# Where the operands of the matrix multiplications lie: all moving ones 192 bytes past all stationary ones, modulo 512

## The chip, the cores and the metric

One NeuronCore of one Trainium2 chip runs the whole kernel. The metric is device time in microseconds (us): before the change 970.22 us, the median of 3 runs (969.55 to 970.27).

## The reference

A small decoder trunk: two layers on a sequence of 256 tokens with 1024 channels, everything in float32. With the sizes of this case (feed-forward width 2816, recurrent width 1280) it computes

```python
h = x
for i in range(2):
    h = h + 0.5 * swiglu(rms_norm(h, ffn1_norm[i]), gate, up, down)     # (silu(x@gate) * (x@up)) @ down
    hn = rms_norm(h, mix_norm[i])
    m = rglru_mixer(hn, ...) if i == 0 else pool_mixer(hn, ...)         # recurrent layer, pooling layer
    h = h + m
    h = h + 0.5 * swiglu(rms_norm(h, ffn2_norm[i]), gate, up, down)
    gate = sigmoid(rms_norm(h, ple_norm[i]) @ ple_w_gate[i])
    h = h + gate * (p[i] @ ple_w_proj[i])
return rms_norm(h, final_norm)
```

Nearly all of the arithmetic is matrix products with weights that are read once: four feed-forward blocks of three 1024 x 2816 products, the in- and out-projections of the recurrent layer, and the two gates of the per-layer input.

## The kernel before

**Layout.** The activations lie transposed, channels on the 128 partitions and the 256 tokens along the free dimension. A weight block of 128 x 128 is the stationary operand of a matmul (TensorE loads it with LDWEIGHTS), a slice of 128 channels x 256 tokens the moving one. The output of 128 x 256 is summed in a PSUM bank.

**Three products for one.** To keep float32 accuracy, each operand is split into a high part in the reduced format float32r and the float32r remainder: `wh`, `wl` for weights, `xh`, `xl` for activations. `mm3` issues three matmuls per block, (wh, xh), (wh, xl), (wl, xh). That gives 7,624 matmuls in float32r; nearly all are of 256 columns. In program order each has its own LDWEIGHTS, and the LDWEIGHTS of the next matmul runs beside the current one. All of them are recorded under one line of a helper, L294.

**The stream of weights.** The weights come as one list of units (`ORDER`), each of 128 partitions x 1024 floats (512 KB). `unit()` hands out the next one and keeps two counters ahead of it: SyncE issues the load of a unit 7 places ahead into a tile `raw` (L261, 5 buffers), and `split` makes its high part (ScalarE, L272) and its low part (VectorE, L273) 4 places ahead in a tile `hl` (6 buffers): the high part of 4096 bytes per partition, then the low one. A unit feeds 24 matmuls.

**The activations.** `Norm.put` writes the split activations into a tile `x` (7 buffers), one for each 256 channels: high and low part, each of two slices of 256 floats. In the feed-forward block the hidden values are split into a tile `hid` (2 buffers of 4096 bytes) and are moving operands of the down products (`acc`). In the recurrent layer `yr` and `ytp` are the two parts of the moving operand of the out-projection (`accl`). `ri` (the gates of the recurrence) is a plain float32 product of weights that are not split.

**Where the buffers lie.** Buffers are laid out one pool behind the other in each partition: constants, `raw`, `hl`, `h` (6 buffers of 2048 bytes), `x`, `st` (small tiles, squares), then the pools of the current stage. The tile `hl` asks for 2 x 1024 + 24 floats, so its pitch is 8288 bytes, 96 past a multiple of 512; the tile `x` asks for 1024 + 8 floats, a pitch of 4128 bytes, 32 past one. Within a tile every operand slice starts at a multiple of 512. By its start modulo 512, then, the allocation gives:

| operand | bytes past a multiple of 512 |
| --- | --- |
| stationary, the 6 buffers of `hl` | 128, 224, 320, 416, 0, 96 |
| moving, the 7 buffers of `x` | 192, 224, 256, 288, 320, 352, 384 |
| moving, `hid`, `yr`, `ytp` | 416 |

This text calls (start of the moving operand minus start of the stationary one) modulo 512 the *offset* of a matmul. It changes with the buffers that meet: in the out-projection the moving operand is always at 416, and the units 0 to 5 of its weights lie in `hl` buffers at 416, 0, 224, 320, 128 and 96, so their 24 matmuls each have the offsets 0, 416, 192, 96, 288 and 320.

**Order of the work.** The order on TensorE is the order of the program: for each normalisation, `project_all` walks over two halves of the channels of several projections; inside it two small float32 sequences are placed by hand, the sums of squares (`ss`, L341, 8 matmuls of one column) and the spreading of the scale over the partitions (`spread`, L378, 4 matmuls). Then the rest of a feed-forward block follows as gate, up and down units without a stop. At the start, 12 float32 matmuls on a tile of ones (`idle`, L241) keep TensorE busy until the first weights are there.

Of the kernel before, what the change touches and what calls it, by code (L numbers as in the profile page):

```python
# [9 lines left out]
F32 = mybir.dt.float32  # L10
F32R = mybir.dt.float32r
# [4 lines left out]
P = 128  # L16
D = 1024
S = 256
# [10 lines left out]
U = 1024  # L29
# [12 lines left out]
    _at += _w  # L42
NV = _at

LINE = 32


def lines(n):
    return -(-n // LINE) * LINE

# [71 lines left out]
def width(key):  # L122
    if key[0] == "lru_gates":
        return min(8, len(GATE_BLOCKS[key[1]]) - 8 * key[2]) * P
    if key[0] == "ple_in":
        return 2 * S
    if key[0] == "pool_op":
        return 4 * (POOL_COLS[key[1]][1] - POOL_COLS[key[1]][0])
    return U
# [81 lines left out]
def trunk(ctx: ExitStack, tc: tile.TileContext, xT, vec, w, out):  # L211
    nc = tc.nc
    PSUM = bass.MemoryType.PSUM
    const = ctx.enter_context(tc.tile_pool(name="const", bufs=1))
    rawp = ctx.enter_context(tc.tile_pool(name="raw", bufs=5))
    hlp = ctx.enter_context(tc.tile_pool(name="hl", bufs=6))
    hp = ctx.enter_context(tc.tile_pool(name="h", bufs=6))
    xp = ctx.enter_context(tc.tile_pool(name="x", bufs=7))
    st = ctx.enter_context(tc.tile_pool(name="st", bufs=1))
# [3 lines left out]
    def narrow(pool, n, dt=F32, **how):  # L223

        return pool.tile([P, lines(n)], dt, **how)[:, :n]

    vt = narrow(const, NV, name="vt")
    nc.scalar.dma_start(vt, vec)
    ones = const.tile([P, P], F32, name="ones")
# [16 lines left out]
    def vcol(name, i):  # L246
        c = VCOL[name] + i
        return vt[:, c:c + 1]
# [15 lines left out]
    def split(n, parts=1):  # L264
        if n not in raws:
            return
        raw = raws.pop(n)
        hl = hlp.tile([P, 2 * U + 24], F32R, tag="hl", name=f"hl{n}")[:, :2 * U].rearrange("p (v u) -> p v u", v=2)
        step = width(ORDER[n]) // parts
        for i in range(parts):  # L270
            c = slice(i * step, (i + 1) * step)
            nc.scalar.activation(hl[:, 0, c], raw[:, c], AF.Copy)  # L272
            nc.vector.tensor_tensor(hl[:, 1, c], raw[:, c], hl[:, 0, c].bitcast(F32), op=ALU.subtract)  # L273
        units[ORDER[n]] = hl

    def unit(*key):
        n = state["used"]
        assert ORDER[n] == key, (ORDER[n], key)
        for what, do, ahead in (("loaded", load, LOADS_AHEAD), ("split", split, SPLITS_AHEAD)):
            while state[what] < min(n + ahead + 1, len(ORDER)):  # L280
                do(state[what])
                state[what] += 1
        state["used"] = n + 1
        return units.pop(key)
# [22 lines left out]
    class Norm:  # L307
# [6 lines left out]
            self.late = None  # L314

        def put(self, j, h, square=True):
            xt = xp.tile([P, 4 * S + 8], F32R, tag="x", name=f"x{self.sid}_{j}")[:, :4 * S].rearrange("p (v c s) -> p v c s", v=2, c=2)
            for c in range(2):
                g = vcol(self.name, 2 * j + c)
                nc.scalar.activation(xt[:, 0, c], h[:, c], AF.Copy, scale=g)  # L320
                nc.vector.scalar_tensor_tensor(  # L321
                    xt[:, 1, c], h[:, c], g, xt[:, 0, c].bitcast(F32), op0=ALU.mult, op1=ALU.subtract)
            self.x[j] = xt
            if square:
                self.square(j, h)
# [505 lines left out]
    load_x(0)  # L831
    load(0, 2)
    split(0, 4)
    load_x(1)
    load(1, 2)
    split(1, 4)
    load(2)
    load(3)
# [39 lines left out]
```

## Time and profile before

| | |
| --- | --- |
| median of 3 runs | 970.22 us |
| profiled execution, whole time | 970.42 us |
| its span, first to last instruction | 968.6 us |
| around the span | 1.8 us |
| TensorE busy | 952.8 us (98%) |
| VectorE, ScalarE, GpSimd busy | 652.1, 491.5, 55.5 us |
[...]
| HBM traffic | 172.4 MB, 178 GB/s over the span |

How to read it: matmuls overlap, since one takes some 280 ns from its start to the end of its drain while the next starts after some 118 ns. So a busy TensorE says only that there was always a matmul in flight; the pace is the distance from one start to the next. A timeline row that merges n matmuls runs from the start of the first to the end of the last; the last start is 0.28 us before that end.

### The profile page before, as it was taken

What the parts mean: (1) busy time and instruction counts of PE and PEld (TensorE: products, weight loads), DVE (VectorE), ACT (ScalarE), POOL (GpSimd) and SP (SyncE); (2) the same over time, 40 slices, a digit from 0 to 9 for tenths busy, and PEclk for the clock granted to TensorE, in tenths of its full rate; (3) what the DMA queues carried; (4) which work ended last, traced back from release to release, by engine and by line L of the source; (5) the groups of instructions that cost most, each with busy time, mean ns of one, the idle gap of its engine ahead of it and who ended that gap; (6) DMA issues with size and microseconds to landing.
All of it is one profiled execution on the core that took longest, in us unless ns stands there. A gap on an engine that the chain in (4) does not pass through costs nothing.

```text
span 968.6 us, 18712 instructions
## 1 busy us (share of the span) xinstructions
PE 952.8 (98%) x7888; PEld 944.8 (98%) x7888; DVE 652.1 (67%) x853; ACT 491.5 (51%) x634; POOL 55.5 (6%) x48
## 2 busy tenths in 40 slices
PE   9999999999999999999999999999989999999997
PEld 8999999999999999999998999999989999999996
DVE  6956555597877755655579855555678855555685
ACT  7544444468785443544456444444448544444443
POOL 1000000023201000000021000000011000000020
PEclk9999999999999999999999999999998999999999
DMA  8866556554435665665545656565524765665611
GB/s 295 286 213 191 182 181 192 169 184 170 153 111 163 209 203 176 196 196 188 183 124 182 208 184 195 167 203 176 185 89 138 251 199 175 197 191 181 193 46 44
DMA packets 49188, 173.63 MB, mean 179 GB/s; under 512 B 5584, under 2 KB 6224, under 8 KB 49104
## 3 DMA queue, kind: packets, MB, share of 16 engines
q1 hardware_dynamic: 48960, 172.29, 55.3%
q8 instruction: 61, 1.00, 0.4%
q14 instruction: 23, 0.19, 0.1%
q10 hardware_dynamic: 144, 0.15, 0.1%
HBM read 171.37 MB, written 1.05 MB: 178 GB/s over the span
## 4 chain that ended last, share of the span: by engine, by line
PE 65%; issue 20%; DVE 9%; ACT 3%; DMA 1%; POOL 0%; SPq 0%; DVEq 0%; ACTq 0%; POOLq 0%
PE up0ffn L294 13%; PE gate0ffn L294 13%; PE acc0ffn L294 12%; PE up1ffn L294 6%; PE gate1ffn L294 6%; PE acc1ffn L294 6%; DVE hl L273 3%; DVE x L321 2%; PE x L294 2%; PE accl L294 1%; PE pp L294 1%; PE ri L294 1%; ACT hl L272 1%; PE ple L294 1%; DMA h<-xT 1%
## 5 line engine op out<-in xcount | busy, mean ns | idle before, releaser
L273 DVE TENSOR_TENSOR hl<-raw,hl 128x1024 fp32r<-128x1024 f32 (+1 forms) x326 | 385.6, 1201 | 234.6 <-ACT hl L272 234.6
L272 ACT ACTIVATE hl<-raw 128x1024 fp32r<-128x1024 f32 (+1 forms) x326 | 332.2, 1036 | 398.9 <-issue 97.2
L294 PE MATMUL gate1ffn<-x,hl 128*128 128x256 f32 x1056 | 130.7, 281 | 2.5 <-DVE x L321 2.2
L294 PE MATMUL gate0ffn<-x,hl 128*128 128x256 f32 x1056 | 130.5, 281 | 0.7 <-ACT hl L272 0.5
L294 PEld LDWEIGHTS gate1ffn<-x,hl 128*128 128x128 f32 x1056 | 127.0, 188 | 3.6 <-DVE x L321 3.0
L294 PE MATMUL up1ffn<-x,hl 128*128 128x256 f32 x1056 | 130.3, 281 | 0.0
L294 PE MATMUL up0ffn<-x,hl 128*128 128x256 f32 x1056 | 129.7, 281 | 0.0
L294 PEld LDWEIGHTS gate0ffn<-x,hl 128*128 128x128 f32 x1056 | 126.9, 189 | 1.5 <-ACT hl L272 0.7
L294 PE MATMUL acc0ffn<-hid,hl 128*128 128x256 f32 x1056 | 128.2, 281 | 0.0
L294 PEld LDWEIGHTS up1ffn<-x,hl 128*128 128x128 f32 x1056 | 127.3, 188 | 0.0
L294 PEld LDWEIGHTS up0ffn<-x,hl 128*128 128x128 f32 x1056 | 127.1, 189 | 0.0
L294 PE MATMUL acc1ffn<-hid,hl 128*128 128x256 f32 x1056 | 126.6, 279 | 0.0
L294 PEld LDWEIGHTS acc0ffn<-hid,hl 128*128 128x128 f32 x1056 | 126.0, 189 | 0.2 <-ACT hid L466 0.2
L294 PEld LDWEIGHTS acc1ffn<-hid,hl 128*128 128x128 f32 x1056 | 124.7, 189 | 0.0
L334 POOL TENSOR_TENSOR sacc<-sq,sq 128x512 f32<-128x512 f32 x9 | 14.7, 1637 | 832.0 <-ACT sq L329 832.0
L321 DVE SCALAR_TENSOR_TENSOR x<-h,vt,x 128x256 fp32r<-128x256 f32 x64 | 48.7, 802 | 7.1 <-ACT x L320 7.0
L294 PE MATMUL ple<-x,hl 128*128 128x256 f32 x384 | 47.2, 282 | 0.0
L294 PEld LDWEIGHTS ple<-x,hl 128*128 128x128 f32 x384 | 46.0, 188 | 0.4 <-DVE x L321 0.2
L466 ACT ACTIVATE hid<-gs 128x512 fp32r<-128x512 f32 x44 | 27.9, 633 | 16.5 <-DVE gs L464 16.5
L320 ACT ACTIVATE x<-h,vt 128x256 fp32r<-128x256 f32 x64 | 28.5, 497 | 5.9 <-DMA vt<-vec 2.7
L464 DVE TENSOR_TENSOR gs<-th,gs 128x512 f32<-128x512 f32 x44 | 30.5, 692 | 1.4
L467 DVE TENSOR_TENSOR hid<-gs,hid 128x512 fp32r<-128x512 f32 x44 | 30.1, 685 | 0.0
(132 smaller groups left out, 688.9 us busy)
## 6 DMA issues: line engine op xcount, KB each, us to landing
raw<-w SPq DMA_DIRECT2D x320, 512.0 KB, 4.2
raw<-w SPq DMA_DIRECT2D x7, 256.0 KB, 4.7
h<-xT SPq DMA_DIRECT2D x4, 256.0 KB, 6.4
out<-hg SPq DMA_DIRECT2D x3, 256.0 KB, 2.8
raw<-w SPq DMA_DIRECT2D x1, 288.0 KB, 2.6
raw<-w SPq DMA_DIRECT2D x2, 128.0 KB, 4.9
out<-hg SPq DMA_DIRECT2D x2, 128.0 KB, 2.0
vt<-vec ACTq DMA_DIRECT2D x1, 148.0 KB, 4.6
```

The source lines that it names most:

```text
L272: nc.scalar.activation(hl[:, 0, c], raw[:, c], AF.Copy)
L273: nc.vector.tensor_tensor(hl[:, 1, c], raw[:, c], hl[:, 0, c].bitcast(F32), op=ALU.subtract)
L294: nc.tensor.matmul(o, lhsT, rhs, start=self.first, stop=self.left == 0, skip_group_check=True)
L320: nc.scalar.activation(xt[:, 0, c], h[:, c], AF.Copy, scale=g)
L321: nc.vector.scalar_tensor_tensor(xt[:, 1, c], h[:, c], g, xt[:, 0, c].bitcast(F32), op0=ALU.mult, op1=ALU.subtract)
L334: nc.gpsimd.tensor_tensor(acc, self.acc, sq, op=ALU.add)
L464: nc.vector.tensor_tensor(gs, th, gs, op=ALU.mult)
L466: nc.scalar.activation(hid[:, 0], gs, AF.Copy)
L467: nc.vector.tensor_tensor(hid[:, 1], gs, hid[:, 0].bitcast(F32), op=ALU.subtract)
```

## The change

The padding goes out of the two tiles, so that both pitches become multiples of 512 (8192 and 4096 bytes), and two small tiles go in: `shift` of 32 bytes in front of the constants, and `apart` of 192 bytes in a pool of its own between `hl` and `h`. GpSimd clears both once. Nothing else of the program differs; no instruction on TensorE, VectorE, ScalarE or SyncE is added, dropped or moved.

```diff
+APART = 48
 ...
     hlp = ctx.enter_context(tc.tile_pool(name="hl", bufs=6))
+    gap = ctx.enter_context(tc.tile_pool(name="gap", bufs=1))
     hp = ctx.enter_context(tc.tile_pool(name="h", bufs=6))
 ...
+    shift = const.tile([P, 8], F32, name="shift")
+    nc.gpsimd.memset(shift, 0.0)
+    apart = gap.tile([P, APART], F32, name="apart")
+    nc.gpsimd.memset(apart, 0.0)
     vt = narrow(const, NV, name="vt")
 ...
-        hl = hlp.tile([P, 2 * U + 24], F32R, tag="hl", name=f"hl{n}")[:, :2 * U].rearrange("p (v u) -> p v u", v=2)
+        hl = hlp.tile([P, 2, U], F32R, tag="hl", name=f"hl{n}")
 ...
-            xt = xp.tile([P, 4 * S + 8], F32R, tag="x", name=f"x{self.sid}_{j}")[:, :4 * S].rearrange("p (v c s) -> p v c s", v=2, c=2)
+            xt = xp.tile([P, 2, 2, S], F32R, tag="x", name=f"x{self.sid}_{j}")
```

## Rows read from the trace of the kernel before

**Rows 1.** The page: busy time by engine, share of the span, instructions.
```profile
PE 952.8 (98%) x7888; PEld 944.8 (98%) x7888; DVE 652.1 (67%) x853; ACT 491.5 (51%) x634; POOL 55.5 (6%) x48
```

**Rows 2.** Stretches, L294 alone: length, PE (matmuls), PEld (loads), clock, DMA, GB/s.
```profile
0.00:34.00 34.00, 26.37 (x211) 25.24 (x212) 1.00 0.85 296
34.00:197.00 163.00, 163.00 (x1380) 162.96 (x1380) 1.00 0.62 196
197.00:290.00 93.00, 92.15 (x692) 88.96 (x692) 1.00 0.44 154
290.00:323.00 33.00, 31.64 (x265) 31.08 (x263) 1.00 0.64 202
323.00:501.00 178.00, 178.00 (x1505) 178.00 (x1506) 1.00 0.58 184
501.00:544.00 43.00, 39.25 (x319) 37.76 (x318) 1.00 0.51 168
544.00:716.00 172.00, 171.80 (x1455) 171.62 (x1454) 1.00 0.58 181
716.00:742.00 26.00, 21.86 (x154) 20.53 (x153) 0.87 0.38 121
742.00:757.00 15.00, 14.09 (x117) 13.70 (x116) 1.00 0.51 169
757.00:929.00 172.00, 171.80 (x1462) 171.62 (x1461) 1.00 0.60 191
929.00:968.60 39.60, 23.07 (x189) 22.30 (x187) 0.95 0.09 28
```

**Rows 3.** Timeline, PE, out-projection: start, length, operation; the second matmul of some mm3.
```profile
277.19 0.28 PE L294 MATMUL accl<-ytp,hl 128*128 128x256 f32 x1
...
280.06 0.28 PE L294 MATMUL accl<-ytp,hl 128*128 128x256 f32 x1
...
282.87 0.28 PE L294 MATMUL accl<-ytp,hl 128*128 128x256 f32 x1
...
285.25 0.28 PE L294 MATMUL accl<-ytp,hl 128*128 128x256 f32 x1
...
285.60 0.28 PE L294 MATMUL accl<-ytp,hl 128*128 128x256 f32 x1
...
288.48 0.28 PE L294 MATMUL accl<-ytp,hl 128*128 128x256 f32 x1
```

**Rows 4.** Timeline, PE: out-projection's unit 5, and 12 matmuls of an up product.
```profile
291.95 0.39 PE L294 MATMUL accl<-ytp,hl 128*128 128x256 f32 x1 [0.52 <-DVE ytp L693]
...
292.41 0.28 PE L294 MATMUL accl<-ytp,hl 128*128 128x256 f32 x1
...
294.89 0.28 PE L294 MATMUL accl<-ytp,hl 128*128 128x256 f32 x1
...
776.20 1.58 PE L294 MATMUL up1ffn<-x,hl 128*128 128x256 f32 x12
```

**Rows 5.** Timeline, PE, windows of several lengths behind ss and behind spread.
```profile
19.81 0.48 PE L294 MATMUL gate0ffn<-x,hl 128*128 128x256 f32 x2
...
19.81 1.61 PE L294 MATMUL gate0ffn<-x,hl 128*128 128x256 f32 x12
...
27.29 0.83 PE L294 MATMUL gate0ffn<-x,hl 128*128 128x256 f32 x5
...
27.29 1.51 PE L294 MATMUL gate0ffn<-x,hl 128*128 128x256 f32 x11
```

**Rows 6.** Stretches with all engines: length, PE, PEld, DVE, ACT, POOL (instructions), clock, DMA, GB/s.
```profile
757.00:929.00 172.00, 172.00 (x1466) 172.00 (x1465) 104.91 (x113) 77.71 (x88) 0.00 (x0) 1.00 0.60 191
```

**Rows 7.** Timeline of the first microseconds, GpSimd and the first weight matmuls.
```profile
0.34 0.10 POOL L870 MEMSET const-uint8-127<- 128x1 uint8 x1
0.73 0.20 POOL L230 MEMSET ones<- 128x128 f32 x1 [0.29 <-POOLq L870]
...
6.60 1.64 PE L294 MATMUL gate0ffn<-x,hl 128*128 128x256 f32 x9 [0.51 <-ACT hl L272]
```

## The prediction

> **What bounds the kernel now.** I read the page's busy times first: TensorE is busy 98% of the span, VectorE 67%, ScalarE 51% [rows 1]. Busy TensorE is no proof of a full pace, because matmuls overlap, so the second view is the table of stretches for L294 alone [rows 2]. It shows four long stretches in which TensorE does nothing but float32r matmuls and never runs dry: 34 to 197, 323 to 501, 544 to 716 and 757 to 929 us. In the last of them VectorE is busy 104.9 of 172 us and ScalarE 77.7 [rows 6], so their work is covered; weights arrive at some 190 GB/s, where the first stretch shows 296 [rows 2]. The kernel is therefore bound by the pace of one matmul behind the other: 163.0 us / 1380 = 118.1 ns, 178.0 / 1505 = 118.3, 171.8 / 1455 = 118.1, 171.8 / 1462 = 117.5. No data wait stands in these, so whatever changes the pace goes straight into the time.
>
> The third view asks whether 118 is one number. The out-projection is an experiment that the kernel makes by itself: same shapes, same moving buffers, one weight buffer after the other, each with its offset. The middle matmuls of the mm3 that open the units stand at 277.19, 280.06, 282.87, 285.60 and 288.48 us [rows 3], so 24 matmuls take
>
> - offset 0: 2.87 us, 119.6 ns each
> - offset 416: 2.81 us, 117.1 ns
> - offset 192: 2.73 us, 113.8 ns; inside the unit, 282.87 to 285.25 is 21 matmuls in 2.38 us, 113.3 ns
> - offset 96: 2.88 us, 120.0 ns.
>
> The spread follows the offset and nothing else that differs between these units. 113.3 is the lowest steady pace that I find anywhere, 120 the highest.
>
> **The catch.** Offset 192 does not always give 113.3. The first 12 up matmuls of a unit at 776.20 also have the offset 192; their last start is at 776.20 + 1.58 - 0.28 = 777.50, so 11 distances take 1.30 us, 118.2 ns [rows 4]. Unit 5 of the out-projection (offset 320, entered after a wait for VectorE) keeps 118.1 over 21 matmuls (292.41 to 294.89) [rows 4]. So at offsets of this kind there are two steady paces, 113.3 and 118, and a stream stays in the one that it came in by: the 12 at 776.20 came from another offset at 118 and did not leave it.
>
> What counts then is how streams enter. Behind the sums of squares, at offset 448 (256 away from 192), the second matmul starts at 20.01 (19.81 + 0.48 - 0.28) and the twelfth at 21.14: ten distances in 1.13 us, 113 ns, from the second matmul on [rows 5]. Behind a spread, at offset 192, the fifth starts at 27.84 and the eleventh at 28.52: six in 0.68 us, 113.3, after four slower ones [rows 5]. Both entries fall into the fast pace. After a wait for data at offset 192 I have no clean case.
>
> **The change part by part.**
>
> *The layout.* The 32 bytes of `shift` move everything behind them from 128 to 160 modulo 512; six `hl` buffers of 8192 keep all weights at 160; with 192 bytes more, `h`, `x`, `st` and the stage pools start at 352. So `x`, `hid`, `yr` and `ytp` meet `hl` at 192 in every buffer. Exceptions, by the code: the projection `pp`, whose moving operand also lies in an `hl` tile (offset 0, 96 matmuls), the pooling product `v` with weights as moving operand (offset 320, 48 matmuls), the narrow `po` (40), and `ri`, which is float32.
>
> *The pace where nothing stops it.* At 113.3 instead of the rows' pace: 4.8 x 1380 = 6.6 us; 5.0 x 1505 = 7.5, less 0.2 for the 48 `pp` among them; 4.8 x 1455 = 7.0; 4.2 x 1462 = 6.1. Sum 27.0 us. These stretches, except the first, begin right behind a spread, the entry that rows 5 show to be fast.
>
> *The pace elsewhere.* From 197 to 290, 692 less 104 `ri` is 588 matmuls; 290 to 323 has 265, 501 to 544 has 319, 742 to 757 has 117, 929 to the end 189 [rows 2]. 1478 x 4.7 = 6.9 us. The stretch from 716 to 742 is left out: clock 0.87, waits for the normalisation and `pp`, `v`, `po`. So is 0 to 34, which waits for data (DMA share 0.85).
>
> *What is given back.* Between the last `ri` and the out-projection's unit 5, 216 matmuls fill the time of the recurrence; TensorE already waits there for VectorE's `ytp`, 0.52 us by the row [rows 4], so 216 x 4.7 = 1.0 us turns into a longer wait. Entries: two for each of eight normalisations and some 15 waits, with 20 ns each until the pace is steady (the four slow distances at 27.29 add about that), 0.6 us. `pp` at offset 0: 96 x 2 ns, 0.2 us. The last spread waits for its chain with 42 matmuls in front, 0.2 us. Sum 2.0 us.
>
> *The two memsets.* They stand ahead of `ones` in GpSimd's queue. Small memsets are recorded as 0.10 us, the one of 128 columns as 0.20 us; each new one has 8 or 48 columns, so 0 to 0.2 us each. `ones` starts at 0.73 and only feeds the warm-up, while the first weight matmul waits for ScalarE until 6.60 [rows 7]; the memsets cost nothing as long as that 5 us cover stands, 0.4 us if it were gone.
>
> *VectorE, ScalarE, DMA.* Their operands move too. The rows give no pair of the same operation at two starts, so I bound this by cover: 104.9 of 172 us means that VectorE's work could grow by half before it sets the pace [rows 6]. With matmuls 4% faster, VectorE's share goes from 61 to 64%. I take 0.
>
> Together: 27.0 + 6.9 - 2.0 = 31.9 us. The profiled execution took 970.42 us (968.6 span and 1.8 around), so 938.5; the median before is 0.2 lower, which changes nothing at this size. I predict 939.
>
> The ends for the unknown, the pace at offset 192 over long stretches: 113.3 and 120.0, the two ends of rows 3. For the 5802 + 1478, some 7,300 matmuls of these stretches, the low end gives the 32 us; the high one 7,300 x (120.0 - 118.0) = 15 us more than before.
>
> [...]
>
> **Rivals.**
>
> *Mixed.* Streams entered after a wait for data fall into 118, those behind `ss` and `spread` into 113.3. For: unit 5 of the out-projection did so, at 320 [rows 4]. Against: no such case at 192. The stretch from 34 to 197 stays as it is (6.6 us), and with it some 350 matmuls between a stage's first wait and its `ss` (1.6 us): 939 + 8.2 = 947. If a fast stream could also drop out in mid-stretch, up to 962.
>
> *Nothing to gain.* Every long stream ends up in the 118 pace, or what the rows show has to do with something other than the offset, or the layout is not what I worked out. The 12 at 776.20 speak for the first, the re-entries against it. 118.0 to 117.8 on 7,300 is 1.5 us: 969.
>
> *Slower.* Weights at 160 and moving operands at 352 meet nowhere in the kernel before as float32r operands. If the conflict depended on absolute starts too, or a disturbed stream could lock into the pace of offset 0, all matmuls would run at 120: 970 + 15 = 985. It decides as soon as the mean distance is above 118.0 + 0.2. Against it: 113.3 was reached at weights starting at 224 and 416 alike (282.87 and 19.81) [rows 3, 5].
>
> **How the numbers follow.** Fast throughout 0.62 (935 to 943 us: 4 us either way for the entries, and for the stretch from 197 to 290, where it depends on VectorE); mixed 0.18 (943 to 962); nothing to gain 0.13 (967 to 972); slower 0.07 (up to 985). About 0.2% is what a measurement of this kernel can tell from no change, here 1.9 us. The first two are faster, with 0.02 of the third: 0.82; same 0.11; slower 0.07. From 934 to 962 lie the first case and nearly all of the second, 8 in 10.
>
> **What would show it.** In the table of stretches the same counts in less time: some 156 us for the 1380 matmuls of the first long stretch, 171, 165 and 166 us for the others. In the timeline, gate and up groups of 48 matmuls take 5.44 us between starts instead of 5.67. If a stretch shows 117.8, its entry went wrong: look at the wait or the `ss` in front of it. If `accl` units still differ among each other, the layout isn't what I worked out. The wait for `ytp` should grow to about 1.5 us. The prediction is wrong if the long stretches stay within 117.5 to 118.3 ns per matmul, or go up to 120.

## The result, and the profile after

The changed kernel takes 960.34 us (median of 4 runs: 956.53, 957.91, 962.77, 963.0) against 970.22: a ratio of 0.990, 95% interval 0.986 to 0.994. The profiled execution took 957.91 us, 12.5 less than the one before. Of the busy times only TensorE's has moved much; the others are within 0.7 us of those of [rows 1].

```profile
PE 937.9 (98%) x7888; PEld 929.7 (97%) x7888; DVE 651.4 (68%) x853; ACT 491.3 (51%) x634; POOL 55.6 (6%) x50
```

The layout is what the change says. The four units of the out-projection that had four paces in [rows 3] now have one: the second matmuls of their first `mm3` are 2.72 us apart each time, 113.3 ns per matmul. Three of these starts:

```profile
269.34 0.28 PE L301 MATMUL accl<-ytp,hl 128*128 128x256 f32 x1
...
272.06 0.28 PE L301 MATMUL accl<-ytp,hl 128*128 128x256 f32 x1
...
274.78 0.28 PE L301 MATMUL accl<-ytp,hl 128*128 128x256 f32 x1
```

But the long stretches, which answer to [rows 2], did not all follow. The columns are length, PE (matmuls), PEld, clock, DMA share, GB/s, for L301 alone (the former L294); the second stretch is shown in two parts.

```profile
35.00:190.00 155.00, 155.00 (x1369) 155.00 (x1369) 1.00 0.64 204
317.00:378.00 61.00, 61.00 (x521) 61.00 (x520) 1.00 0.59 183
387.00:489.00 102.00, 102.00 (x903) 102.00 (x902) 1.00 0.62 197
534.00:703.00 169.00, 169.00 (x1437) 169.00 (x1436) 1.00 0.57 181
746.00:917.00 171.00, 171.00 (x1454) 171.00 (x1453) 1.00 0.59 187
```

Divide length by matmuls: 113.2 ns in the first stretch, 117.1 and then 113.0 in the second, 117.6 in the third and fourth. (Such a quotient comes out a little low, since matmuls that only overlap the ends are counted; starts in the timeline give 113.3 and 117.8.) Every operand lies as in the first stretch, the clock is 1.00, no wait stands in any of them, and yet there are two paces. From here on *fast* is 113.3 and *slow* 117.8 at offset 192.

The entries tell the stretches apart. All but the first begin behind a spread; this is the one at 314.88 us:

```profile
314.88 0.60 PE L385 MATMUL spread<-dg,ones 128*128 128x128 f32 x4
315.24 1.66 PE L301 MATMUL up0ffn<-x,hl 128*128 128x256 f32 x12
316.74 1.58 PE L301 MATMUL gate0ffn<-x,hl 128*128 128x256 f32 x12
```

The last 12 matmuls take 1.58 - 0.28 = 1.30 us for 11 distances, 118.2 ns: the stream came in slow and stayed so for the 528 matmuls up to the `pp`. Behind these 48, which have offset 0, the timeline has

```profile
382.77 2.08 PE L301 MATMUL pp<-hl,hl 128*128 128x256 f32 x16
384.69 5.63 PE L301 MATMUL gate0ffn<-x,hl 128*128 128x256 f32 x48
390.15 2.09 PE L301 MATMUL up0ffn<-x,hl 128*128 128x256 f32 x17
```

48 matmuls in 390.15 - 384.69 = 5.46 us, 113.8 ns with the first few in it: the same stream is fast now and stays fast to the end of the stretch.

Summed from the starts in the trace, 7,487 regular distances (100 to 140 ns between two neighbouring matmuls of L301, `po` left out) fell from 883.4 to 867.7 us (118.0 to 115.9 ns), and what lies between them (waits, entries, float32 matmuls) grew by 2.9 us. These two make up the 12.5 us to within 0.3.

### The profile page after: what moved, and what is told of

It reads as the page before. It is cut to its first block, busy times and chain, and to the rows that moved or that the text cites. A ratio compares the mean times of both kernels' runs of the same rounds, so it can differ in the third digit from the quotient of the medians.

```text
span 956.0 us, 18714 instructions
## 1 busy us (share of the span) xinstructions
PE 937.9 (98%) x7888; PEld 929.7 (97%) x7888; DVE 651.4 (68%) x853; ACT 491.3 (51%) x634; POOL 55.6 (6%) x50
## 4 chain that ended last, share of the span: by engine, by line
PE 64%; issue 21%; DVE 11%; ACT 3%; DMA 0%; POOL 0%; DVEq 0%; ACTq 0%; POOLq 0%
PE up0ffn L301 13%; PE gate0ffn L301 13%; PE acc0ffn L301 12%; PE up1ffn L301 6%; PE gate1ffn L301 6%; PE acc1ffn L301 6%; DVE hl L280 3%; DVE x L328 2%; PE x L301 2%; PE accl L301 1%; PE pp L301 1%; PE ri L301 1%; ACT hl L279 1%; PE xb L301 1%; DVE t L517 1%
## 5 line engine op out<-in xcount | busy, mean ns | idle before, releaser
L280 DVE TENSOR_TENSOR hl<-raw,hl 128x1024 fp32r<-128x1024 f32 (+1 forms) x326 | 385.2, 1199 | 228.1 <-ACT hl L279 228.0
L279 ACT ACTIVATE hl<-raw 128x1024 fp32r<-128x1024 f32 (+1 forms) x326 | 332.3, 1036 | 384.2 <-issue 93.0
L301 PE MATMUL gate1ffn<-x,hl 128*128 128x256 f32 x1056 | 130.1, 281 | 3.0 <-DVE x L328 2.4
L301 PEld LDWEIGHTS gate1ffn<-x,hl 128*128 128x128 f32 x1056 | 126.5, 189 | 4.0 <-DVE x L328 3.2
L301 PE MATMUL up1ffn<-x,hl 128*128 128x256 f32 x1056 | 129.5, 281 | 0.0
L301 PE MATMUL acc1ffn<-hid,hl 128*128 128x256 f32 x1056 | 127.6, 281 | 0.0
L301 PE MATMUL gate0ffn<-x,hl 128*128 128x256 f32 x1056 | 126.7, 278 | 0.2
L301 PEld LDWEIGHTS up1ffn<-x,hl 128*128 128x128 f32 x1056 | 126.4, 189 | 0.0
L301 PEld LDWEIGHTS acc1ffn<-hid,hl 128*128 128x128 f32 x1056 | 125.8, 189 | 0.0
L301 PE MATMUL up0ffn<-x,hl 128*128 128x256 f32 x1056 | 125.4, 277 | 0.0
L301 PE MATMUL acc0ffn<-hid,hl 128*128 128x256 f32 x1056 | 124.2, 277 | 0.0
L301 PEld LDWEIGHTS gate0ffn<-x,hl 128*128 128x128 f32 x1056 | 123.3, 188 | 0.8 <-DVE x L328 0.3
L301 PEld LDWEIGHTS up0ffn<-x,hl 128*128 128x128 f32 x1056 | 122.8, 188 | 0.0
L301 PEld LDWEIGHTS acc0ffn<-hid,hl 128*128 128x128 f32 x1056 | 122.1, 188 | 0.3 <-ACT hid L473 0.2
L301 PE MATMUL ple<-x,hl 128*128 128x256 f32 x384 | 45.6, 278 | 0.2 <-DVE x L328 0.2
L301 PEld LDWEIGHTS ple<-x,hl 128*128 128x128 f32 x384 | 44.4, 188 | 0.5 <-DVE x L328 0.4
```

Source lines behind the costliest of these rows:

```text
L301: nc.tensor.matmul(o, lhsT, rhs, start=self.first, stop=self.left == 0, skip_group_check=True)
```

## The experiments

Each kernel is the changed one with the edit shown, timed beside the kernel before on the same chip (medians 969.96 to 970.47 us). Where a single time is given, the kernel ran once, profiled.

**again: the changed kernel once more.** Do the paces belong to the program or to the run? No edit.

> The changed kernel once more, unaltered. Theory A (at offset 192 there are two steady paces, 113.3 and 117.8 ns, and a stream keeps the one it entered by until something disturbs it): each long stretch is again wholly at one of the two, and which one may differ from the first profile where the stretch begins with a wait for data; the time differs from the first one by whole stretches, some 6.1 us for each of about 1370 to 1450 matmuls. Theory B (the pace is fixed by the offset of each matmul, the rest is chance): the long stretches have the same pace as in the first profile or one in between, and single distances of 113 and 118 ns are mixed.

956.96 us. From 60 to 180 us the trace has 1061 matmuls in 120 us, from 560 to 680 and 770 to 890 us 1021 each: the first stretch fast, the second slow and then fast, the third and fourth slow, as in the profile after. So the pattern of the long stretches repeats here. Two lines, 60 to 180 and 560 to 680 us:

```profile
60.00:180.00 120.00, 120.00 (x1061) 120.00 (x1061) 1.00 0.62 194
560.00:680.00 120.00, 120.00 (x1021) 120.00 (x1020) 1.00 0.60 186
```

**kick96: disturb the streams.** If a stream merely stays in the pace by which it came in, a short stretch with another offset should let it come in again. Twelve units, three in each feed-forward block, lie 96 bytes higher in their buffers: offset 96 for 24 matmuls each, which costs some 24 x 6.7 ns per unit.

```diff
+def moved(key):
+    return 24 if key[0] in ("ffn1", "ffn2") and key[2:] in (("up", 1, 1), ("gate", 3, 0), ("gate", 7, 0)) else 0
 ...
-        hl = hlp.tile([P, 2, U], F32R, tag="hl", name=f"hl{n}")
+        k = moved(ORDER[n])
+        hl = hlp.tile([P, 2 * U + 128], F32R, tag="hl", name=f"hl{n}")[:, k:k + 2 * U].rearrange("p (v u) -> p v u", v=2)
```

> As the changed kernel, but 12 of the 327 weight units (three in each feed-forward block: the last one in front of the gap-free stretch, one of pair 3, one of pair 7) lie 96 bytes further on, so their 24 matmuls each have the offset 96, whose pace is 120 ns. In the kernel before, a stream that came from offset 96 into 192 was at 113.3 within some three matmuls in all cases. Theory A: all four gap-free stretches run at 113.3; from 957.9 us of the first profile, 528 + 1440 + 1452 slow matmuls x 4.45 ns = 15.2 us less, 12 x 24 x 6.7 ns = 1.9 us more: 944.6 us, between 942 and 948, and the runs agree better than those of the changed kernel. Theory B: only the 288 moved matmuls change, 1.9 us more than the changed kernel: 958 to 965 us.

946.97 us (944.17 to 948.81), ratio 0.975 (0.972 to 0.978). In the windows 330 to 370, 560 to 680 and 770 to 890 us:

```profile
330.00:370.00 40.00, 40.00 (x341) 40.00 (x340) 1.00 0.58 187
560.00:680.00 120.00, 120.00 (x1059) 120.00 (x1058) 1.00 0.60 190
770.00:890.00 120.00, 120.00 (x1059) 120.00 (x1058) 1.00 0.61 191
```

1059 in 120 us is 113.3. The third and fourth stretches turned fast, by an edit that moves 12 of some 320 units by 96 bytes; only the first part of the second came back slow each time. Theory A, that a stream keeps its pace until it has to come in again, holds, and its rival falls: the same stretch, with the same work of the other engines around it, runs at either pace. That a stream from 96 into 192 is always fast does not hold here, and did not in the kernel before: of three entries of that kind there, the one at 740.36 us stayed at 117.8.

**kick160: the direction of the kick.** The same with 32 bytes (offset 160), which I expected to leave slow streams slow.

```diff
-    return 24 if key[0] in ("ffn1", "ffn2") and key[2:] in (("up", 1, 1), ("gate", 3, 0), ("gate", 7, 0)) else 0
+    return 8 if key[0] in ("ffn1", "ffn2") and key[2:] in (("up", 1, 1), ("gate", 3, 0), ("gate", 7, 0)) else 0
```

> The same 12 units, but 32 bytes further on in place of 96: offset 160, with a pace of 117 ns. In the kernel before, every stream that came from 160 into 192 stayed at 117.8. Theory A: all four gap-free stretches run at 117.8 from the moved units on; the changed kernel's fast ones, 1370 matmuls from 35 to 190 us and 912 from 386 to 489 us, lose 4.45 ns each less what lies before the moved unit: 966 to 969 us, 22 us over the kernel with 96 bytes. Theory B: 288 matmuls at 117, as the changed kernel, 957 to 963 us, and within 3 us of the kernel with 96 bytes.

947.16 us (945.52 to 948.7), ratio 0.976 (0.974 to 0.978): a miss by 20 us. All four long stretches are fast (1060, 1058 and 1060 matmuls from 60 to 180, 560 to 680 and 770 to 890 us), the second from its first marked unit (354 matmuls from 330 to 370 us, 113.0 ns), the third and fourth from their second; a stream that was fast came back fast from every kick. That a re-entry keeps the side on which the stream was, as I had read the 12 matmuls in [rows 4], is refuted.

**kick208.** The same with 496 bytes (124 floats, offset 208).

```diff
-    return 24 if key[0] in ("ffn1", "ffn2") and key[2:] in (("up", 1, 1), ("gate", 3, 0), ("gate", 7, 0)) else 0
+    return 124 if key[0] in ("ffn1", "ffn2") and key[2:] in (("up", 1, 1), ("gate", 3, 0), ("gate", 7, 0)) else 0
```

> The 12 weight units of the two earlier runs, now at offset 208 (24 matmuls each at 117.8 ns), which in the scan had one pace only and was followed by 113.3 at 448 in one case. Theory A (a stream keeps the pace it came in by, and the unit ahead can turn it): if 208 wipes out what came before, all gap-free stretches are at 113.3 from the first moved unit on: 957 - 15.2 + 12 x 24 x 4.45 ns = 943 us, 941 to 946. If the exit from 208 falls into 117.8, all of them are slow behind a moved unit: 966 to 969.

954.41 us (946.74 to 957.05), ratio 0.983 (0.977 to 0.988): above the expectation, though the profiled run, 946.74, is in line with it and shows all stretches fast but the first part of the second (342 matmuls from 330 to 370 us). What the three longer runs did was not profiled. A kick does not work each time: in the long stretches of the three profiles a slow stream came out of a kick fast 2 times of 4 (offset 96), 3 of 5 (160) and 2 of 4 (208). Whether that depends on the offset is not shown.

**scan: the pace of every offset.** Each group of nine unit positions of the feed-forward blocks gets another shift, 36 in all, in steps of 16 bytes and four near 192.

```diff
+    g = 9 * (2 * l + (which == "ffn2")) + (p if m == "down" else p - 2)
 ...
+    return 4 * g if g < 32 else (126, 2, 127, 1)[g - 32]
```

> As the changed kernel, but in the feed-forward blocks the weight units of each group of 144 matmuls lie 16 bytes further on than those of the group before: 36 groups pass through all 32 offsets 192, 176, 160, ... 208 in steps of 16, and then 200, 184, 196, 188. It measures the steady pace at each offset. Theory A: groups at 64, 192, 320, 448 are at 113.3 or 117.8, at 0 and 256 at 120.0, at 96 and 352 near 120; 16 bytes to the side of 192 the pace should lie between. Is there an offset with 113.3 or less that has no slow pace? Theory B gives the same list of paces, but one value for each offset, 113.3 at 192.

969.44 us. The timeline gives each pace between two groups of 48:

```profile
334.58 5.76 PE L312 MATMUL gate0ffn<-x,hl 128*128 128x256 f32 x48
340.18 5.76 PE L312 MATMUL up0ffn<-x,hl 128*128 128x256 f32 x48
...
464.78 5.61 PE L312 MATMUL up0ffn<-x,hl 128*128 128x256 f32 x48
470.22 5.87 PE L312 MATMUL acc0ffn<-hid,hl 128*128 128x256 f32 x48
...
790.39 5.92 PE L312 MATMUL up1ffn<-x,hl 128*128 128x256 f32 x48
796.15 5.84 PE L312 MATMUL acc1ffn<-hid,hl 128*128 128x256 f32 x48
```

5.60 us for 48 is 116.7 ns at offset 48; 5.44 is 113.3 at offset 448; 5.76 is 120.0 at offset 256. All of them, ns per matmul:

| offset | pace | offset | pace |
| --- | --- | --- | --- |
| 0, 256 | 120.0 | 144, 400 | 120.0 |
| 16, 272 | 120.0 | 160; 416 | 118.6; 117.3 |
| 32, 288 | 116.7 | 176, 432 | 118.8 |
| 48, 304 | 116.7 | 184; 188 | 118.3 |
| 64, 320 | 117.8 | 192, 448 | 113.3 (or 117.8) |
| 80, 336 | 118.1 | 196; 200 | 119.5; 117.8 |
| 96, 352 | 120.0 | 208, 464 | 117.8 |
| 112, 368 | 120.0 | 224, 480 | 118.3 |
| 128, 384 | 118.6 | 240, 496 | 118.3 |

The pattern repeats every 256 bytes, not 512, with one exception, 160 and 416; and of these offsets only 192 modulo 256 reaches 113.3; four bytes beside it (188 and 196) the pace is 118.3 and 119.5. Each offset was passed once, so a second pace at others than 192 could have been missed; 160 and 416 look like one.

**off0 and off32: the whole kernel at another offset.**

```diff
-APART = 48
+APART = 128     # off0;  off32: APART = 8
```

> The gap is 512 bytes in place of 192: every float32r matmul at offset 0. In the scan and in the kernel before 0 had one steady pace, 120.0 ns. Theory A: all stretches at 120.0: 970.4 + 7300 x 2.0 ns = 985 us, 983 to 987. Theory B (the common pitch helped): 957 to 963.

984.1 us, within the expectation: the same number of instructions, 1002 matmuls in 120 us. This is the price of the slower rival, which the prediction put at 985.

```profile
604.25 5.92 PE L301 MATMUL up1ffn<-x,hl 128*128 128x256 f32 x48
610.01 5.92 PE L301 MATMUL acc1ffn<-hid,hl 128*128 128x256 f32 x48
```

> The gap is 32 bytes in place of 192: every float32r matmul at offset 32. In the scan 32 had one steady pace, 116.67 ns. Theory A: no second pace, so the runs agree as well as those of the kernel before (within some 0.2%), and all regular matmuls are at 116.67: 970.4 - 7300 x (118.0 - 116.67) = 9.7 us less, 960 to 962 us. Theory B (what helped is the common pitch, not the offset): 957 to 963 with the spread of the changed kernel.

963.51 us (962.3 to 965.54), ratio 0.993 (0.991 to 0.996): some 2 us above the expectation. The pace is 116.7 in the long stretches but for the 925 matmuls behind `pp`, which run at 117.8 (as do three short stretches):

```profile
400.00:480.00 80.00, 80.00 (x682) 80.00 (x681) 1.00 0.58 186
560.00:680.00 120.00, 120.00 (x1030) 120.00 (x1030) 1.00 0.60 189
```

80 / 682 is 117.3 against 120 / 1030 = 116.5 by the same quotient. So 32 has a second pace too, worth 925 x 1.1 ns = 1.0 us here; the other 1 us I can't place.

**ones320: is it the offset of the small float32 matmuls?** The tile `ones`, the stationary operand of the spread, moves back to where it was relative to the moving operands in the kernel before (theory C).

```diff
+    pad1 = const.tile([P, 104], F32, name="pad1")
     ones = const.tile([P, P], F32, name="ones")
 ...
+    pad2 = const.tile([P, 24], F32, name="pad2")
 ...
```

> As the changed kernel, but the tile of ones, the stationary or moving operand of the float32 sequences ss and spread, lies 416 bytes further on, with a pad behind it, so that ss and spread have the offsets 480 and 32 again that they had in the kernel before (64 and 448 in the changed one); all float32r matmuls keep 192. Theory C (a stream takes its pace from how the last matmuls of ss or spread leave the engine, which their own offset sets): behind spread the long stretches from 316, 533 and 745 us now come in at 113.3, as the one at 27.29 us in the kernel before, and behind ss at 113.3 too: some 3600 of the 4056 slow matmuls x 4.45 ns = 15 us less than the changed kernel, 941 to 944 us. Theory D (their offset has no part in it, the float32r layout alone decides): as the changed kernel, 956 to 963 us.

960.22 us (945.12 to 963.51). C is refuted by the profiled run, 963.51: the entries behind a spread in the feed-forward blocks are still slow (342 matmuls from 330 to 370 us, 1021 each from 560 to 680 and 770 to 890 us, as in the changed kernel). It even has the first stretch slow:

```profile
60.00:180.00 120.00, 120.00 (x1021) 120.00 (x1021) 1.00 0.60 187
```

That also gives a reading of the spread of the times: one long stretch more or less at the slow pace is some 1,380 x 4.5 ns = 6.2 us, and the changed kernel's four runs lie at 956.5 to 957.9 and at 962.8 to 963.0. That its two longer runs had the first stretch slow is inferred; they were not profiled. Nor was the run of 945.12 us here, 18.4 less than the profiled one, which at 4.45 ns each is some 4,100 matmuls turned fast, most of the long stretches: which pace a long stretch takes can then differ between runs of one program.

**spread6: is it the place of the spread within a unit?** In the feed-forward blocks the spread goes to the boundary between two units (theory E).

```diff
 ...
-    h, norm = ffn(1, "ffn1", h, norm, "mix_norm1")
+    h, norm = ffn(1, "ffn1", h, norm, "mix_norm1", spread_at=6)
 ...
```

The three other blocks are changed alike.

> As the changed kernel, but in the four feed-forward blocks the four matmuls of spread are issued 12 matmuls later, between two weight units in place of the middle of one; layout and number of instructions are the same. In all profiles so far the stream behind these four spreads came in at 117.8 ns, behind those of the other stages mostly at 113.3. Theory E (the place, that is which operands follow, decides the entry): the entries change, and where they come in at 113.3 the stretches from 317, 534 and 745 us lose 528, 1440 and 1452 x 4.45 ns: 942 to 951 us if all three or two of them turn. Theory F (something else of these stages decides): all three stay at 117.8, 956 to 963 us.

950.11 us (945.75 to 951.49), ratio 0.979 (0.976 to 0.982), and E is refuted all the same: the entries are still slow. What helps is that TensorE's loads now wait 0.16 us for `hid` some 8 us behind the spread, and that the stream comes out of them fast in the second and third stretches:

```profile
324.17 0.54 PEld L301 LDWEIGHTS acc0ffn<-hid,hl 128*128 128x128 f32 x4 [0.16 <-ACT hid L473]
...
319.46 2.99 PE L301 MATMUL up0ffn<-x,hl 128*128 128x256 f32 x24
322.29 1.93 PE L301 MATMUL gate0ffn<-x,hl 128*128 128x256 f32 x15
...
333.71 5.60 PE L301 MATMUL up0ffn<-x,hl 128*128 128x256 f32 x48
339.15 1.07 PE L301 MATMUL acc0ffn<-hid,hl 128*128 128x256 f32 x8
```

24 in 322.29 - 319.46 = 2.83 us, 117.9 ns; later 48 in 5.44, 113.3. From 560 to 680 us, in the third stretch, there are 1062 matmuls. The fourth has the same wait at 746.5 us and stayed slow behind it (1021 from 770 to 890 us).

**spread3: is it the length of the float32 sequence?** The first product of each spread is issued twice, with the same result: 6 small matmuls in a row instead of 4 (theory H).

```diff
-            ps = accp.tile([P, S], F32, tag="acc", name=f"spread{self.sid}")
+            ps, dgs = accp.tile([P, S], F32, tag="acc", name=f"spread{self.sid}"), []
 ...
-                nc.tensor.matmul(ps[:, t * P:(t + 1) * P], ones, dg, start=t == 0, stop=t == 1, skip_group_check=True)
+                dgs.append(dg)
+            for t in (0, 0, 1):
+                nc.tensor.matmul(ps[:, t * P:(t + 1) * P], ones, dgs[t], start=t == 0, stop=t == 1, skip_group_check=True)
```

> As the changed kernel, but the first of the two products of each spread is issued twice, six small matmuls in place of four, some 0.2 us more each time. Theory H (the length and rhythm of the float32 sequence decide how a stream enters): the entries behind spread in the four feed-forward blocks, at 117.8 in every profile so far, turn to 113.3 in some or all of them. Theory F (something else of these stages decides): they stay at 117.8, and those of the other stages mostly at 113.3.

944.69 us: 12 to 13 us less than the two profiled runs of the changed kernel, by adding work. All seven entries behind a spread come in fast. The one that stood at 314.88 above:

```profile
314.58 0.83 PE L387 MATMUL spread<-dg,ones 128*128 128x128 f32 x6
315.17 1.62 PE L301 MATMUL up0ffn<-x,hl 128*128 128x256 f32 x12
316.63 1.64 PE L301 MATMUL gate0ffn<-x,hl 128*128 128x256 f32 x13
```

1.64 - 0.28 = 1.36 us for 12 distances, 113.3 ns. H holds in this run: in the feed-forward blocks, 4 of 4 with six small matmuls against 0 of 32 with four (eight profiles at offset 192: the changed kernel twice, the kicks, ones320, spread6). But four don't always lead to the slow pace: at the three other places, 19 of 24 entries in these profiles come in fast. There the four mostly wait for their second product (0.44 us from the first start to the stream's, 0.36 in the feed-forward blocks); two that did not wait came in fast too, so this is not the whole rule. Why a sequence leads in fast or slow isn't settled.

**scan_wl: can the slow pace be taken away?** As in the scan, but only the low part of the weights moves, so that of the three matmuls of `mm3` two keep the offset 192 and the third has another.

```diff
-        hl = hlp.tile([P, 2, U], F32R, tag="hl", name=f"hl{n}")
+        k = moved(ORDER[n])
+        hl = Pair(hlp.tile([P, 2 * U + 128], F32R, tag="hl", name=f"hl{n}"), U + k)
```

`moved` is that of the scan; `Pair`, shown with the next experiment, gives the low part a start of its own.

> As the changed kernel, but in the feed-forward blocks the low half of the weights lies 16 bytes further on from group to group of 144 matmuls (the high half stays), so in every third matmul, the one in which the low half is loaded beside it, the offset passes through all of 192, 176, ... 208. Theory A (the pace comes from the offset of the running matmul and of the load beside it): the pace changes from group to group by at most a third of what the scan of both halves showed, between 113.3 and 118.7 ns; where the 117.8 pace at 192 has no counterpart, a group has one pace only, whatever came before. If a group is below 113.3 or always at it, its layout is a better one. Rival (only the common pitch matters): all groups stay at the pace of the group before.

961.33 us. The pace changes from group to group, so it isn't fixed by the entry of the whole stream, which was the rival. Groups whose third matmul has the offset 64 or 320 (128 modulo 256 away from 192) run at 113.3 throughout, out of neighbours at 116.9; at 184 it is 115.6, at 208 and 464 116.7, elsewhere mostly 117.8 to 118.9 (448, which is 192 again modulo 256, has 113.3). The step from 336 to 320, 117 to 113.3:

```profile
643.07 5.78 PE L321 MATMUL up1ffn<-x,hl 128*128 128x256 f32 x48
648.68 5.60 PE L321 MATMUL acc1ffn<-hid,hl 128*128 128x256 f32 x48
654.12 5.60 PE L321 MATMUL gate1ffn<-x,hl 128*128 128x256 f32 x48
```

**wl128 and wl8: two of these for the whole kernel.** The low part of every unit lies 128 (8) bytes higher.

```diff
+LOW = 32     # wl8: LOW = 2
+class Pair:
+    def __init__(self, t, low):
+        self.t, self.low = t, low
+    def __getitem__(self, at):
+        _, v, c = at
+        return self.t[:, v * self.low + c.start:v * self.low + c.stop]
 ...
-        hl = hlp.tile([P, 2, U], F32R, tag="hl", name=f"hl{n}")
+        hl = Pair(hlp.tile([P, 2 * U + 128], F32R, tag="hl", name=f"hl{n}"), U + LOW)
```

> As the changed kernel, but the low half of every weight unit lies 128 bytes further on, so two of three matmuls have the offset 192 and the third, beside which a low half is loaded, 64. In the scan of the low half both groups of this kind (64 and 320) were wholly at 113.3, coming from groups at 116.9. Theory G (this layout has the pace of 113.3 alone): all regular matmuls at 113.3 however a stream enters, 4056 x 4.45 = 18 us less than the first profile of the changed kernel: 938 to 941 us, the time that was forecast, and the runs agree within 0.2%. Theory A' (two paces here too, those groups entered by luck): stretches at 113.3 and 117.8 as in the changed kernel, 945 to 963 us.

941.54 us (941.32 to 942.69), ratio 0.971 (0.968 to 0.973): the best version, and the steadiest, within 1.4 us over four runs. Every long stretch is fast:

```profile
36.00:189.00 153.00, 153.00 (x1352) 153.00 (x1351) 1.00 0.64 203
317.00:376.00 59.00, 59.00 (x523) 59.00 (x522) 1.00 0.59 189
387.00:487.00 100.00, 100.00 (x885) 100.00 (x884) 1.00 0.62 196
532.00:694.00 162.00, 162.00 (x1432) 162.00 (x1431) 1.00 0.60 188
738.00:901.00 163.00, 163.00 (x1440) 163.00 (x1440) 1.00 0.61 194
```

112.8 to 113.2 ns by the quotient, 113.3 by starts; whatever the entry, the pace is there within some ten matmuls (behind the spread at 315.25 us the first 11 distances take 1.35 us, and from 317 us on the pace is that of the second line above).

> As the changed kernel, but the low half of every weight unit lies 8 bytes further on: two of three matmuls at 192, the third at 184. In the scan of the low half this group was at 115.6 ns throughout. Theory G: one pace, 115.6, in all stretches, 970.4 - 7300 x 2.4 ns = 953 us, 951 to 955. Theory A': several paces, by the stretch.

956.07 us, 1 us above the expectation; the single pace of 115.6 stands throughout:

```profile
770.00:890.00 120.00, 120.00 (x1041) 120.00 (x1040) 1.00 0.60 189
```

**kicks5: more kicks.** Five moved units per feed-forward block instead of three, with mixed offsets.

```diff
+KICKS = {("up", 1, 1): 24, ("gate", 2, 1): 8, ("up", 3, 0): 124, ("gate", 4, 1): 24, ("up", 6, 0): 8}
```

> As the changed kernel, but five weight units of each feed-forward block lie off 192 by 96, 32, 496, 96 and 32 bytes, one pair apart. In the runs with 12 such units, a stream at 113.3 came back to 113.3 behind such a unit each time, and one at 117.8 came out at 113.3 in about half of the cases. Theory A: with five tries of three kinds nearly every gap-free stretch ends at 113.3, so the runs agree better than those with three tries of one kind: 957 - 15.2 + 20 x 24 x 5 ns = 944 us, 942 to 949 in every run. Theory B (no memory of a pace): 288 more matmuls off 192 than there, 958 to 966 us.

947.45 us (946.06 to 949.28), ratio 0.977 (0.975 to 0.980), as expected but for one run 0.3 us above it: all long stretches fast soon behind their entry (1057 matmuls each from 60 to 180, 560 to 680 and 770 to 890 us, kicks included). wl128 does the same for nothing.

The times follow the mean of the regular distances (7,472 to 7,489 of them, by kernel), with an exception for what waits take back. The last column is what is left from TensorE's first matmul to its last:

| kernel | mean pace, ns | regular matmuls, us | the rest, us |
| --- | --- | --- | --- |
| before | 117.99 | 883.4 | 77.3 |
| off0 | 119.97 | 897.6 | |
| off32 | 116.88 | 873.6 | |
| after | 115.90 | 867.7 | 80.2 |
| kick96 | 114.42 | 855.3 | |
| spread3 | 113.76 | 851.9 | |
| wl128 | 113.50 | 848.1 | 84.7 |

## Why the prediction was right or wrong

**Right: what bounds the kernel, and the direction.** The pace in the long stretches is what the time follows. 984.1 us at offset 0 and 941.5 at 192 with the low part moved come from the same instructions in the same order.

**Right: the pace at 192.** 113.3 was read from 21 matmuls [rows 3]; it holds over 1,369.

**The step that failed: "These stretches, except the first, begin right behind a spread, the entry that rows 5 show to be fast."** One fast entry in [rows 5] was taken for the rule. In the changed kernel the entries behind a spread in the four feed-forward blocks came in slow, in this profile, in its repeat and in those of the kicks and of ones320 and spread6. Even the entry that was fast at 27.29 us in the kernel before, with the offset 192 there too, is slow now. It and the entries of the third and fourth stretches:

```profile
26.67 1.66 PE L301 MATMUL gate0ffn<-x,hl 128*128 128x256 f32 x12
...
532.50 1.66 PE L301 MATMUL up1ffn<-x,hl 128*128 128x256 f32 x12
...
744.87 1.66 PE L301 MATMUL up1ffn<-x,hl 128*128 128x256 f32 x12
```

Each has 11 distances in 1.38 us; the first is 0.20, so the other ten take 118 ns each. The kernel before held a warning. By the addresses of its allocation it has 29 series of 10 to 24 matmuls at offset 192 or 448: 14 settle at 113.3 and 15 stay near 117.8. Of the 14 that lie inside its long stretches 13 stay slow; the prediction weighed one of these, the 12 at 776.20, against the entries of [rows 5].

Stretch by stretch, from the starts (boundaries by number of matmul, which differ a little from the prediction's):

| long stretch | predicted gain, us | after | wl128 |
| --- | --- | --- | --- |
| first | 6.6 | 6.7 | 6.6 |
| second | 7.3 | 4.7 | 7.1 |
| third | 7.0 | 0.5 | 7.2 |
| fourth | 6.1 | -0.4 | 6.0 |
| sum | 27.0 | 11.5 | 26.9 |

The last column is the prediction's sum once the second pace is gone: its sizes were right, and the entries were what it lacked. Of the 31.9 us forecast the profiled run gained 12.5; the long stretches account for 15.5 of the 19.4 that are missing. The median of the runs gained less, 9.9 us, since two of them took some 6 us longer; that the first stretch was slow in these is inferred, as said above.

**A second term mis-sized: "the pace elsewhere", 6.9 us, less 2.0 given back.** Even in wl128 everything outside the long stretches gained 0.8 us (27.7 in all, less 26.9), not 4.9. The mean pace of the whole kernel is 113.5 ns in wl128, but the stages from 197 to 323 us and around the normalisations wait for VectorE and ScalarE (in wl128 1.9 us for `ytp`, 2.8 for the `x` of `v`, 3.1 for that of `gate1ffn`). From 197 to 323 us, where 4.0 us less 1.0 were forecast, the changed kernel gained 0.5 (some of its matmuls ran slow there too) and wl128 lost 0.1. In wl128 the regular distances gained 35.3 us (1.7 of them because 15 fewer count as regular) and the rest grew by 7.4. One of these waits the prediction had named: that for `ytp`, 0.52 us in [rows 4], to grow to about 1.5. Columns: total, times, longest; the second line is wl128's.

```profile
PE accl L301 <- DVE ytp L700: 1.5, 1, 1.5
...
PE accl L313 <- DVE ytp L712: 1.9, 1, 1.9
```

It did, and in wl128 more was lost behind it: the granted clock was 0.50 for 13 matmuls, at some 213 ns each, 1.3 us more. The line is for 284.30 to 287.20 us, in the columns of the stretches:

```profile
284.30:287.20 2.90, 2.90 (x13) 2.90 (x14) 0.50 0.79 250
```

The other waits are small, but there are many: all of TensorE's together grew from 8.7 us to 10.9 in the changed kernel and 12.7 in wl128. A gain in a stage that waits for another engine's chain should have been put at nothing.

**The rivals.** *Mixed* had the outcome, in its outer range (up to 962), with the sides exchanged: it let the entries after a wait fall slow and those behind a spread fast. Most entries after a wait came in fast (in the profile after 7 of 9, of those with a recorded wait and 14 matmuls or more behind it; spread6 shows one), and those behind a spread in the feed-forward blocks slow. The case that the prediction had for it, unit 5 of the out-projection, was none: its offset 320 is 64 modulo 256, which ran at 117.8 in the scan with no wait in front. *Nothing to gain* and *slower* fall: 120.0 comes with other offsets (0 in off0), and 1,369 matmuls with starts at 160 against 352 ran at 113.3.

**The memsets** cost nothing: `ones` starts 0.11 us later, and the first weight matmul at 6.45 instead of 6.60 us [rows 7].

```profile
0.84 0.20 POOL L237 MEMSET ones<- 128x128 f32 x1
```

**VectorE and ScalarE** at nothing was right: VectorE's split of a unit takes 1199 ns, 1201 before, ScalarE's 1036 in both.

## What to carry to other kernels

When a kernel is bound by the distance from one matmul to the next, measure that distance stage by stage and by the addresses of its operands, and try the layout as a whole at a few offsets: here 43 us lie between the worst and the best for the same instructions. A steady pace read from twenty matmuls says what is possible, not what a stream will take: where a short stretch of before shows two paces under equal conditions, forecast the mixture, or look for a layout that has only one. Speed that is gained in a stage that waits for another engine can come back as a longer wait: here that for `ytp` went from 0.5 to 1.5 and, in wl128, 1.9 us.

## What the runs showed of the hardware that was not expected

- At offset 192 modulo 256 the stream of float32r matmuls, each with its own load, has two steady paces, 113.3 and 117.8 ns, and keeps the one it took for over 1,400 matmuls with nothing to tell them apart in the trace.
- What ran just ahead can pick the pace: in the feed-forward blocks 4 small float32 matmuls led to 117.8 in 32 of 32 entries, 6 to 113.3 in 4 of 4 (one run). The rule behind it stays open, as does what decides behind the other spreads, the sums of squares and waits, where both occur (fast 19 of 24 behind the other spreads in eight profiles; in the profile after 3 of 7 behind sums of squares and 7 of 9 behind waits).
- In the scan the pace went with the distance of the two operands modulo 256 bytes, from 113.3 to 120.0 ns, but for one pair (160: 118.6, 416: 117.3), and 4 bytes changed it (192: 113.3, 196: 119.5). A second pace is not a matter of 192 alone: in off32 there are 116.7 and 117.8. Whether the weights in use or those being loaded beside them count is not told apart.
- With every third matmul at offset 64 and the others at 192, only 113.3 was seen where the granted clock was 1.00 and nothing waited, apart from the `pp`, although 64 alone gives 117.8.
- In wl128 the 13 matmuls behind the wait for `ytp` (1.9 us) ran at the granted clock 0.50, 213 ns each. Behind the same wait of 0.5 us before and 1.5 us in the changed kernel the clock was 1.00. That the longer wait lowered it is inferred.
